# Bidirectional hybrid encoder, two layers on one core: the SSD's heads begun evenly over the short conv's triples, and the FFN's normalized input made pair by pair between the scaled pairs

## The chip, the cores and the metric

The kernel runs on one core of a Trainium2 chip. A core has five engines, each with a queue of its own that it works through in order: TensorE (PE in the profile, with its weight loads shown as PEld), VectorE (DVE), ScalarE (ACT), GpSimd (POOL) and SyncE (SP), which here only issues DMAs. Engines wait for one another through semaphores. The metric is the device time of one execution in microseconds. Three runs of the kernel before gave 796.75 to 798.28 us, with a median of 798.2 us.

## The reference, cut to what matters

The sequence has 256 tokens of 1024 features; there are two layers, and everything is float32.

```python
for l in range(2):
    n = rms_norm(h, norm1_w[l])
    z, xbc, dt_f, dt_b, sc_b, sc_c, sc_v = split(n @ w_in[l])
    y_ssd = ssd_branch(z, xbc, dt_f, dt_b, ...)      # 16 heads in 4 groups, forward and backward, gated, group norm
    y_sc  = sc_b * dwconv3(sc_c * sc_v, sc_conv_w[l])  # the short conv
    h = h + concat(y_ssd, y_sc) @ w_out[l]
    n = rms_norm(h, norm2_w[l])
    g, u = split(dwconv3(n @ w_ffn_up[l]) + ffn_conv_b[l])   # 2816 columns each
    h = h + (silu(g) * u) @ w_ffn_down[l]
out = rms_norm(h, final_norm_w)
```

## The kernel before

Activations lie with features on the 128 partitions and the 256 tokens along the row. Every large product is made from three matmuls: the operands are split into a high and a low part in the engine's reduced float32 (`hilo`, L101 to L103: ACT writes the high part, DVE subtracts it for the low part), and high x high, low x high and high x low are added up in PSUM. Weights come as chunks of 128x1024: SP loads one into a `raw` buffer, ACT makes `wh` (L102), DVE makes `wl` (L103), four chunks ahead of use; there are seven buffers of `wh` and `wl`, so a chunk's split waits until PE has used the seventh before it. 128 matmul columns of an input projection are one half of a **pair**; a pair has 48 matmuls of 256 columns, works off two chunks (24 matmuls each: the first uses input features 0 to 511, the second 512 to 1023), and fills one of four PSUM banks named `mm`.

**The norm.** RMSNorm needs the sum over all features before its factor `rs` is known. So the first pairs of each projection are multiplied from the unnormalized input times the norm's weight (`hwh`, `hwl`), and their result is scaled afterwards by DVE (`take`, which writes `u`); these are the scaled pairs. Once `rs` is there, `normed` makes the normalized input: for each of four feature pairs p, two DVE multiplications `nf` of 128x256, one ACT cast `nh` and one DVE subtraction `nl` of 128x512. Pairs from index NU = 5 on (6 in the first layer's mixer) take `nh` and `nl`. In an FFN, pairs 0 to 2 lie around the computation of `rs`, pairs 3 and 4 are scaled pairs too, and pair 5 is the first that reads `nh` and `nl`. `Norm.some` makes one feature pair; it is also handed to `pair` as `between`, which calls it behind each half of a scaled pair. In the kernel before, `scale` empties `left` at once for all norms but the first layer's mixer, and the later calls of `some` find nothing to do. Each FFN pair has two column blocks, gate and up: `conv` (one ACT and two DVE instructions each, `cacc`), a SiLU `sg` on ACT, and the product `af` on DVE.

**The mixer's second half.** The short conv's twelve pairs come as four triples (c, v, b). Beside them DVE and ACT work on the SSD's 16 heads; `HEADS_AT` is made from the table `_STARTS`, which names for each head the slot at which it begins, with two slots to a pair (2n + 1 for pair n) and, from 24 on, one slot to each chunk of the output projection. Four heads make a group: the first one of a group issues its transposes and score products on PE (`xp`, `sp`), each head makes its decay matrix `m` on DVE, and HEAD_LAG = 4 slots behind the group's last head PE multiplies (`py`). Then DVE adds up the group (L723 to L730) and splits its square sum (`sqx`), and NORM_LAG = 4 slots later PE sums it over the partitions (`gt`), which the group's norm needs.

**The order.** A scheduler lays the instructions of each engine in a row from the program's order and its own estimate of when each is ready. On the engine, that row is fixed.

Of the kernel before, what the change touches and what calls it, by code (L numbers as in the profile page):

```python
# [42 lines left out]
DT_BASE = 3072  # L43


_STARTS = (1, 3, 3, 7, 9, 11, 11, 15, 17, 19, 19, 21, 21, 23, 24, 24)
HEADS_AT = {_n: _STARTS.count(_n) for _n in _STARTS}
HEAD_LAG = 4
NORM_LAG = 4
# [17 lines left out]
def hybrid_trunk(ctx: ExitStack, tc: tile.TileContext, xT, w_in, w_dt, w_out, w_up, w_dn,  # L67
# [100 lines left out]
    def chunk():  # L168
        while len(split) < min(len(plan), pos[0] + 1 + AHEAD):
            issue()  # L170
        got = split[pos[0]]
        split[pos[0]] = None
        pos[0] += 1
        return got
# [30 lines left out]
    def begin():  # L205
# [29 lines left out]
        for q in range(4):  # L235
            if q > 1:
                square(q - 2)
            hi, lo = parts("hwh"), parts("hwl")
            for j in range(2):
                if q == 0 and j == 0:  # L240
                    raw, wh, _ = w(0, 0)
                    put(v, v.tensor_copy(wh, raw))
                scale = x0[:, 2 * q + j:2 * q + j + 1]
                put(s, s.activation(hi[:, j, :], h[q][:, j, :], AF.Identity, scale=scale))
                put(v, v.scalar_tensor_tensor(out=lo[:, j, :], in0=h[q][:, j, :], scalar=scale,
                                              in1=hi[:, j, :].bitcast(F32), op0=ALU.mult, op1=ALU.subtract))
                xs.append((hi[:, j, :], lo[:, j, :]))
            for i in range(BEGIN):
                raw, wh, wl = w(i, q)
                if q or i:  # L250
                    put(s, s.copy(wh, raw))
                put(v, v.tensor_tensor(out=wl, in0=raw, in1=wh.bitcast(F32), op=ALU.subtract))
            if q == 1:

                gate = const.tile([P, 1], F32, name="gate")
                put("pool", nc.gpsimd.tensor_copy(gate, lo[:, 1, 0:1].bitcast(F32)))
# [33 lines left out]
    def scaled(l):  # L290

        for i, (name, n) in enumerate(NORMS.items()):
            w = x0[:, 0:KD] if l == 0 and name == "n1" else pars[l][:, COL[name]:COL[name] + 8]
            a = s.activation(wn[l][:, i], w, AF.Identity, scale=-0.5 / n)
            if l:
                after(a, tab["uses"][-1])
# [8 lines left out]
    def products(ps, wts, xs, first, last, js=None):  # L305

        wh, wl, kc, cols = wts
        for kk in range(kc):
            xh, xl = xs[kk]
            for j in js or range(cols // P):  # L310
                o = kk * cols + j * P
                a, b = wh[:, o:o + P], wl[:, o:o + P]
                f = first and kk == 0
                e = last and kk == kc - 1
                te.matmul(ps[:, j, :], a, xh, start=f and j == 0, stop=False, skip_group_check=True)
                te.matmul(ps[:, j, :], a, xl, start=False, stop=False, skip_group_check=True)
                te.matmul(ps[:, j, :], b, xh, start=False, stop=e, skip_group_check=True)

    def first_pairs(xs):

        ps = [ps_mm.tile([P, 2, L], F32, name="mm") for _ in range(BEGIN)]
        wts = [[chunk(), chunk()] for _ in range(BEGIN)]
        for q in range(4):
            for ab in (((0, 0), (0, 1)), ((1, 0),)):
                for i, (a, b) in ((i, x) for i in range(BEGIN) for x in ab):
                    for k in (2 * q, 2 * q + 1):
                        for j in range(2):
                            o = k % KC * 256 + j * P
                            te.matmul(ps[i][:, j, :], wts[i][k // KC][a][:, o:o + P], xs[k][b],
                                      start=k == 0 and j == 0 and a == b, stop=k == KD - 1 and a == 1, skip_group_check=True)  # L330
        return ps

    def pair(xs, between=lambda k: None):
        ps = ps_mm.tile([P, 2, L], F32, name="mm")
        n = len(xs)
        for k in range(0, n, KC):
            products(ps, chunk(), xs[k:k + KC], k == 0, k + KC >= n)
            between(k)
        return ps
# [11 lines left out]
    def exact(sq):  # L351

        t = k2("sqx", F32R)
        hilo(sq, t[:, 0, :], t[:, 1, :])
        return t[:, 0, :], t[:, 1, :]

    def halves_sum(sq):
        r = k1("sqh")
        v.tensor_tensor(out=r, in0=sq[:, 0, :], in1=sq[:, 1, :], op=ALU.add)
        return r  # L360

    def rstd(sq, n, name, sq_on):

        tot = bank(name)[:, 0, :]
        for i, x in enumerate(sq):
            te.matmul(tot, ones_r, x, start=i == 0, stop=i == 1)
        r = tmp.tile([P, L], F32, name="rs1") if name == "tot" else k1("grs")
        return newton(tot, n, k1("ry"), k1("rt"), r, sq_on)
# [13 lines left out]
    def weighted(l, name, pairs):  # L382

        xs = []
        for p in pairs:
            hi, lo = parts("hwh"), parts("hwl")
            for j in range(2):
                w = pc(l, name, 2 * p + j)
                s.activation(hi[:, j, :], h[p][:, j, :], AF.Identity, scale=w)
                v.scalar_tensor_tensor(out=lo[:, j, :], in0=h[p][:, j, :], scalar=w,  # L390
                                       in1=hi[:, j, :].bitcast(F32), op0=ALU.mult, op1=ALU.subtract)
                xs.append((hi[:, j, :], lo[:, j, :]))
        return xs
# [13 lines left out]
    class Norm:  # L407
# [10 lines left out]
        def begin(self, pairs):  # L418
            self.raw += weighted(self.l, self.name, pairs)
            for p in pairs:  # L420
                self.sq = squares(p, h[p], self.sq)

        def scale(self):
            if self.l == 0 and self.name == "n1":
                scaled(0)
            self.r = rstd(exact(halves_sum(self.sq)), D, "tot", v)
            self.full, self.left = [], [0, 1, 2, 3]
            if self.l or self.name != "n1":
                while self.left:
                    self.some()  # L430

        def some(self, go=True):

# [13 lines left out]
        def pairs(self, extra=None):  # L447

            first = self.rest is None

            def more():
                if extra is not None:
                    for k in range(0, KD, KC):
                        extra(k)
            if first:
                ps = first_pairs(self.raw)
                more()
                ps += [pair(self.raw, lambda k: self.scale() if k == 0 else self.some())]
            else:

                ps = [ps_mm.tile([P, 2, L], F32, name="mm") for _ in range(2)]
                for i, c in ((0, 0), (1, 0), (0, 1), (1, 1)):
                    if (i, c) == (1, 1):
                        more()
                    products(ps[i], chunk(), self.raw[KC * c:KC * c + KC], c == 0, c == 1)
                    if (i, c) == (0, 0):
                        self.rest()
                        self.begin((2, 3))
                if extra is not None:
                    self.scale()  # L470
                else:
                    ps += [pair(self.raw, lambda k: self.scale() if k == 0 else None)]
            for x in ps:
                yield self.take(x, True)
            nu = NU_FIRST if first else NU
            for n in itertools.count(len(ps)):
                yield self.take(pair(self.raw, self.some) if n < nu else pair(self.full), n < nu)

    def across(acc, x, wts, c, half, first=False):
# [485 lines left out]
```

## Time and profile before

| | before |
|---|---|
| median of three runs | 798.2 us (796.75 to 798.28) |
| the profiled execution's own time | 797.5 us |
| its span, first to last instruction | 795.7 us |
| PE busy | 785.3 us (99%) |
| DVE busy | 652.6 us (82%) |
| ACT busy | 536.6 us (67%) |

The times that follow count from the start of the span. A matmul's length in the profile overlaps the next one's; what PE spends on a run of matmuls is best read from the chain, as start and length of the whole run. Two DVE instructions that don't wait overlap by about 0.08 us in the profile as well, so a row of them costs its length less that much each.

### The profile page before, as it was taken

How to read it: one execution, taken by the hardware profiler on the slowest of the kernel's cores; microseconds unless marked ns; L12 is line 12 of the kernel's file. 1: busy time of each engine (PE TensorE's matmuls, PEld its weight loads, DVE VectorE, ACT ScalarE, POOL GpSimd, SP SyncE). 2: the span in 40 equal slices, each digit the busy share in tenths (PEclk: the TensorE clock that was granted, in tenths of full speed). 3: DMA queues.
4: the chain of work that ended last, by engine and by line, in shares of the span. 5: the costliest groups of instructions: out<-in, count | busy, mean ns of one | idle time of the engine just before them, and what ended most of it. 6: DMA issues, size and time to landing. Idle time of an engine off the chain costs nothing.

```text
span 795.7 us, 14870 instructions
## 1 busy us (share of the span) xinstructions
PE 785.3 (99%) x5730; PEld 742.9 (93%) x5730; DVE 652.6 (82%) x1106; ACT 536.6 (67%) x962; POOL 39.0 (5%) x68
## 2 busy tenths in 40 slices
PE   9999999999999999999999999999999999999996
PEld 9999999978999999999899999999889999999995
DVE  7997879998699977777599778899968999777773
ACT  7866968986766655555577679789747665555552
POOL 1002201100000000000000102101000000000000
PEclk9999999999999999999999999999999999999998
DMA  8568676556454776655373876656656348565531
GB/s 293 192 202 309 175 248 213 174 161 232 123 180 134 245 227 188 185 186 185 113 238 100 257 240 207 215 183 188 185 181 202 117 160 263 187 185 186 185 107 54
DMA packets 47463, 151.31 MB, mean 190 GB/s; under 512 B 9104, under 2 KB 9936, under 8 KB 47392
## 3 DMA queue, kind: packets, MB, share of 16 engines
q1 hardware_dynamic: 39680, 138.98, 54.3%
q0 software_dynamic: 7424, 10.99, 4.8%
q8 instruction: 45, 0.74, 0.4%
q10 hardware_dynamic: 288, 0.39, 0.1%
q14 instruction: 26, 0.21, 0.1%
HBM read 149.14 MB, written 1.15 MB: 189 GB/s over the span
## 4 chain that ended last, share of the span: by engine, by line
PE 92%; DVE 5%; ACT 1%; issue 1%; DMA 0%; DVEq 0%; ACTq 0%
PE mm L95 72%; PE dn L95 15%; PE py L95 2%; DVE wl L103 1%; DVE nf L398 1%; PE sp L95 1%; ACT wh L102 1%; PE warm L95 1%; PE tr L99 1%; DVE w L649 0%; DMA raw<-in_w_out_dram 0%; PE dtp L95 0%; DVE nl L103 0%; PE xp L99 0%; DVE m L651 0%
## 5 line engine op out<-in xcount | busy, mean ns | idle before, releaser
L102 ACT CAST wh<-raw 128x1024 fp32r<-128x1024 f32 (+1 forms) x259 | 267.6, 1039 | 175.8 <-PE mm L95 99.7
L103 DVE TENSOR_TENSOR wl<-raw,wh 128x1024 fp32r<-128x1024 f32 (+1 forms) x257 | 311.8, 1216 | 86.3 <-ACT wh L102 86.1
L95 PE MATMUL mm<-nh,wh 128*128 128x256 f32 x1136 | 323.1, 284 | 0.0
L95 PE MATMUL mm<-nh,wl 128*128 128x256 f32 x1136 | 321.5, 283 | 0.0
L95 PE MATMUL mm<-nl,wh 128*128 128x256 f32 x1136 | 321.4, 283 | 0.0
L95 PEld LDWEIGHTS mm<-nl,wh 128*128 128x128 f32 x1136 | 217.8, 192 | 1.4
L95 PEld LDWEIGHTS mm<-nh,wh 128*128 128x128 f32 x1136 | 217.7, 192 | 1.4
L95 PEld LDWEIGHTS mm<-nh,wl 128*128 128x128 f32 x1136 | 217.8, 192 | 0.1
L95 PE MATMUL mm<-hwh,wh 128*128 128x256 f32 x336 | 91.9, 285 | 0.9 <-DVE u L444 0.9
L95 PE MATMUL mm<-hwl,wh 128*128 128x256 f32 x336 | 91.2, 283 | 0.0
L95 PE MATMUL mm<-hwh,wl 128*128 128x256 f32 x336 | 90.5, 283 | 0.0
L95 PE MATMUL dn<-wh,acth 128*128 128x512 f32 x176 | 69.1, 392 | 0.0
L95 PE MATMUL dn<-wh,actl 128*128 128x512 f32 x176 | 68.9, 391 | 0.0
L95 PE MATMUL dn<-wl,acth 128*128 128x512 f32 x176 | 68.5, 389 | 0.0
L95 PEld LDWEIGHTS mm<-hwh,wh 128*128 128x128 f32 x336 | 62.6, 192 | 1.4 <-PE mm L95 1.3
L95 PEld LDWEIGHTS mm<-hwl,wh 128*128 128x128 f32 x336 | 62.3, 190 | 0.1
L95 PEld LDWEIGHTS mm<-hwh,wl 128*128 128x128 f32 x336 | 62.1, 190 | 0.0
L95 PE MATMUL mm<-wh,mixh 128*128 128x512 f32 x128 | 50.5, 395 | 0.7 <-DVE sy L794 0.7
L95 PE MATMUL mm<-wl,mixh 128*128 128x512 f32 x128 | 49.9, 390 | 0.0
L95 PE MATMUL mm<-wh,mixl 128*128 128x512 f32 x128 | 49.9, 390 | 0.0
L516 DVE SCALAR_TENSOR_TENSOR cacc<-mm,pars,cacc 128x255 f32<-128x255 f32 x88 | 42.0, 477 | 4.6 <-ACT cacc L515 4.4
L518 DVE SCALAR_TENSOR_TENSOR cacc<-mm,pars,cacc 128x255 f32<-128x255 f32 x88 | 42.3, 481 | 2.4
(177 smaller groups left out, 936.7 us busy)
## 6 DMA issues: line engine op xcount, KB each, us to landing
raw<-in_w_in_dram SPq DMA_DIRECT2D x91, 512.0 KB, 4.4
raw<-in_w_up_dram SPq DMA_DIRECT2D x88, 512.0 KB, 3.9
raw<-in_w_dn_dram SPq DMA_DIRECT2D x44, 512.0 KB, 3.6
raw<-in_w_out_dram SPq DMA_DIRECT2D x32, 512.0 KB, 4.2
bc<-dcs POOLq DMA_DIRECT2D x32, 256.0 KB, 5.5
raw<-in_w_in_dram SPq DMA_DIRECT2D x10, 256.0 KB, 5.1
er<-der POOLq DMA_DIRECT2D x16, 128.0 KB, 5.9
h<-in_xT_dram SPq DMA_DIRECT2D x3, 256.0 KB, 5.7
```

Source lines behind the costliest of these rows:

```text
L95: cls.put(nc.tensor.matmul(*args, **kw))
L99: cls.put(nc.tensor.transpose(*args))
L102: s.copy(hi, full)
L103: v.tensor_tensor(out=lo, in0=full, in1=hi.bitcast(F32), op=ALU.subtract)
L398: v.scalar_tensor_tensor(out=n[:, j, :], in0=h[p][:, j, :], scalar=wc(l, name, 2 * p + j), in1=r, op0=ALU.mult, op1=ALU.mult)
L516: v.scalar_tensor_tensor(out=acc[:, 1:L], in0=u[:, 0:L - 1], scalar=w0, in1=acc[:, 1:L], op0=ALU.mult, op1=ALU.add)
L518: v.scalar_tensor_tensor(out=acc[:, 0:L - 1], in0=u[:, 1:L], scalar=w2, in1=acc[:, 0:L - 1], op0=ALU.mult, op1=ALU.add)
```

## The change

The table of starts is replaced by one in which the heads begin evenly, the last at slot 21 in place of 24. And `scale` no longer empties `left`: the normalized pairs are made by the calls of `some` between the halves of the scaled pairs, with a loop that makes what is left before the first full pair.

```diff
-_STARTS = (1, 3, 3, 7, 9, 11, 11, 15, 17, 19, 19, 21, 21, 23, 24, 24)
+_STARTS = (1, 3, 3, 5, 7, 7, 9, 11, 11, 13, 15, 15, 17, 19, 19, 21)
...
             self.full, self.left = [], [0, 1, 2, 3]
-            if self.l or self.name != "n1":
-                while self.left:
-                    self.some()
...
             nu = NU_FIRST if first else NU
             for n in itertools.count(len(ps)):
+                if n >= nu:
+                    while self.left:
+                        self.some()
                 yield self.take(pair(self.raw, self.some) if n < nu else pair(self.full), n < nu)
```

The number of matmuls and of DMAs stays as it was, and SP's queue is the same row for row. What moves is shown at three places.

**The first FFN, DVE, behind `rs`.** Before, the four normalized pairs stand right behind the norm's factor, and the first `u` behind the third `nl`:

```order
L379 SCALAR_TENSOR_TENSOR rs_3050<-rt,ry 128x256
L398 SCALAR_TENSOR_TENSOR nf<-x_84,wn_90,rs_3050 128x256 x2
L398 SCALAR_TENSOR_TENSOR nf<-h_85,wn_90,rs_3050 128x256 x2
L103 TENSOR_TENSOR nl<-nf,nh 128x512
L398 SCALAR_TENSOR_TENSOR nf<-h_86,wn_90,rs_3050 128x256
L103 TENSOR_TENSOR nl<-nf,nh 128x512
L398 SCALAR_TENSOR_TENSOR nf<-h_86,wn_90,rs_3050 128x256
L398 SCALAR_TENSOR_TENSOR nf<-h_87,wn_90,rs_3050 128x256 x2
L103 TENSOR_TENSOR nl<-nf,nh 128x512
L444 SCALAR_TENSOR_TENSOR u<-mm,rs_3050 128x512
```

Now the first `u` stands right behind `rs`, and the FFN's own work on pairs 0 to 2 follows, with five weight chunks among it:

```order
L379 SCALAR_TENSOR_TENSOR rs_3050<-rt,ry 128x256
L441 SCALAR_TENSOR_TENSOR u<-mm,rs_3050 128x512
L103 TENSOR_TENSOR wl<-raw,wh 128x1024
L516 SCALAR_TENSOR_TENSOR cacc<-u,pars_88,cacc 128x255 x2
L518 SCALAR_TENSOR_TENSOR cacc<-u,pars_88,cacc 128x255 x2
L103 TENSOR_TENSOR wl<-raw,wh 128x1024
L856 SCALAR_TENSOR_TENSOR af<-cacc,pars_88,sg 128x256
L441 SCALAR_TENSOR_TENSOR u<-mm,rs_3050 128x512 x2
L103 TENSOR_TENSOR wl<-raw,wh 128x1024
L516 SCALAR_TENSOR_TENSOR cacc<-u,pars_88,cacc 128x255 x2
L518 SCALAR_TENSOR_TENSOR cacc<-u,pars_88,cacc 128x255 x2
L103 TENSOR_TENSOR wl<-raw,wh 128x1024
```

**The same row of DVE, a little further on**, directly behind the piece above (of the second `af` to the second pair's `nl`):

```order
L856 SCALAR_TENSOR_TENSOR af<-cacc,pars_88,sg 128x256
L516 SCALAR_TENSOR_TENSOR cacc<-u,pars_88,cacc 128x255 x2
L103 TENSOR_TENSOR actl<-af,acth 128x512
L518 SCALAR_TENSOR_TENSOR cacc<-u,pars_88,cacc 128x255 x2
L103 TENSOR_TENSOR wl<-raw,wh 128x1024
L856 SCALAR_TENSOR_TENSOR af<-cacc,pars_88,sg 128x256
L398 SCALAR_TENSOR_TENSOR nf<-x_84,wn_90,rs_3050 128x256 x2
L398 SCALAR_TENSOR_TENSOR nf<-h_85,wn_90,rs_3050 128x256 x2
L103 TENSOR_TENSOR nl<-nf,nh 128x512
L441 SCALAR_TENSOR_TENSOR u<-mm,rs_3050 128x512
L103 TENSOR_TENSOR nl<-nf,nh 128x512
```

The first `nl` has moved behind three `u`, twelve `cacc`, three `af`, one `actl` and five `wl`. The third one follows that piece after another 13 instructions: three more `nf` with the first of them ahead of four `cacc`, an `af`, a `u`, a `wl`, an `actl` and one `cacc`:

```order
L398 SCALAR_TENSOR_TENSOR nf<-h_86,wn_90,rs_3050 128x256
L516 SCALAR_TENSOR_TENSOR cacc<-u,pars_88,cacc 128x255 x2
L518 SCALAR_TENSOR_TENSOR cacc<-u,pars_88,cacc 128x255 x2
L398 SCALAR_TENSOR_TENSOR nf<-h_86,wn_90,rs_3050 128x256
L856 SCALAR_TENSOR_TENSOR af<-cacc,pars_88,sg 128x256
L398 SCALAR_TENSOR_TENSOR nf<-h_87,wn_90,rs_3050 128x256 x2
L441 SCALAR_TENSOR_TENSOR u<-mm,rs_3050 128x512
L103 TENSOR_TENSOR wl<-raw,wh 128x1024
L103 TENSOR_TENSOR actl<-af,acth 128x512
L516 SCALAR_TENSOR_TENSOR cacc<-u,pars_88,cacc 128x255
L103 TENSOR_TENSOR nl<-nf,nh 128x512
```

On ACT, the last two `nh` now stand behind the split of the chunk `wh` that needs the buffer of pair 5's first half:

```order
L139 ACTIVATE sg<-cacc,pars_88 128x256
L102 CAST wh<-raw 128x1024
L102 CAST acth<-af 128x512
L515 ACTIVATE cacc<-u,pars_88 128x256 x2
L102 CAST nh<-nf 128x512 x2
```

**The first mixer, DVE, the last group's square sum.** Before, the rows ahead of the last but one group's `sqx` (x_1081 and x_1153 are the third and fourth group's sums) read:

```order
L103 TENSOR_TENSOR wl<-raw,wh 128x1024
L730 TENSOR_TENSOR sq<-sq 128x256
L723 TENSOR_TENSOR yo<-py,er 128x256
L724 SCALAR_TENSOR_TENSOR x_1153<-x_1153,pars_88,py 128x256
L723 TENSOR_TENSOR yo<-py,er 128x256
L726 TENSOR_TENSOR x_1153<-x_1153,yo 128x256
L103 TENSOR_TENSOR sqx<-sq,sqx 128x256
```

Now the last group's stands there:

```order
L103 TENSOR_TENSOR wl<-raw,wh 128x1024
L726 TENSOR_TENSOR x_1153<-x_1153,yo 128x256
L103 TENSOR_TENSOR wl<-raw,wh 128x1024
L727 TENSOR_TENSOR x_1153<-x_1153,z_859 128x512
L103 TENSOR_TENSOR wl<-raw,wh 128x1024
L730 TENSOR_TENSOR sq<-sq 128x256
L103 TENSOR_TENSOR wl<-raw,wh 128x1024 x2
L103 TENSOR_TENSOR sqx<-sq,sqx 128x256
```

On PE, the product `gt` that needs this last `sqx` now comes two matmuls (one `gt`) behind the place where the third group's came before; in between lies the same work. The second layer's mixer and FFN have the same rows at these places.

## Rows read from the trace of the kernel before

**Rows 1.** The page, busy time, share of the span and count of each engine.

```profile
PE 785.3 (99%) x5730; PEld 742.9 (93%) x5730; DVE 652.6 (82%) x1106; ACT 536.6 (67%) x962; POOL 39.0 (5%) x68
```

**Rows 2.** The waits of PE: for whom, us in total, times, longest.

```profile
PE gt L95 <- ACT sqx L102: 1.1, 1, 1.1
...
PE mm L95 <- DVE u L444: 0.9, 2, 0.5
PE mm L95 <- DVE sy L794: 0.7, 1, 0.7
```

**Rows 3.** The chain that ended last, pieces by start and length: PE's runs.

```profile
83.55 0.44 PE xp L99 x4
...
233.23 17.49 PE mm L95 x144
...
412.69 63.35 PE mm L95 x528
...
623.31 17.51 PE mm L95 x144
```

**Rows 4.** The timeline of DVE in the first FFN: start, length, line, instruction.

```profile
226.95 0.42 DVE L379 SCALAR_TENSOR_TENSOR rs<-rt,ry 128x256 f32<-128x256 f32 x1
227.41 0.88 DVE L398 SCALAR_TENSOR_TENSOR nf<-x,wn,rs 128x256 f32<-128x256 f32 x2
...
229.00 0.69 DVE L103 TENSOR_TENSOR nl<-nf,nh 128x512 fp32r<-128x512 f32 x1
...
232.39 0.69 DVE L444 SCALAR_TENSOR_TENSOR u<-mm,rs 128x512 f32<-128x512 f32 x1
...
233.59 1.22 DVE L103 TENSOR_TENSOR wl<-raw,wh 128x1024 fp32r<-128x1024 f32 x1
234.73 0.88 DVE L516 SCALAR_TENSOR_TENSOR cacc<-u,pars,cacc 128x255 f32<-128x255 f32 x2
...
237.74 0.48 DVE L856 SCALAR_TENSOR_TENSOR af<-cacc,pars,sg 128x256 f32<-128x256 f32 x1 [0.21 <-ACT sg L139]
...
243.71 0.69 DVE L103 TENSOR_TENSOR actl<-af,acth 128x512 fp32r<-128x512 f32 x1
```

**Rows 5.** The timeline of ACT in the first FFN.

```profile
228.33 0.62 ACT L102 CAST nh<-nf 128x512 fp32r<-128x512 f32 x1 [0.28 <-DVE nf L398]
...
245.88 1.05 ACT L102 CAST wh<-raw 128x1024 fp32r<-128x1024 f32 x1 [1.49 <-DMA raw<-in_w_up_dram]
246.96 0.91 ACT L515 ACTIVATE cacc<-u,pars 128x256 f32<-128x256 f32 x2
...
251.03 0.61 ACT L102 CAST acth<-af 128x512 fp32r<-128x512 f32 x1
```

**Rows 6.** The chain's first pieces: PE's first matmuls.

```profile
1.06 5.07 PE warm L95 x22
```

**Rows 7.** Windows: the two mixers' second halves in two parts each, and the end.

```profile
core 0: us, PE busy (x) PEld busy (x) DVE busy (x) ACT busy (x) POOL busy (x), PEclk, DMA share, GB/s
101.00:135.80 34.80, 34.80 (x293) 34.29 (x292) 28.65 (x54) 26.26 (x58) 4.37 (x7) 1.00 0.71 228
135.80:179.80 44.00, 42.25 (x300) 37.15 (x298) 43.65 (x98) 37.82 (x89) 4.68 (x8) 1.00 0.57 180
488.70:528.00 39.30, 39.30 (x333) 38.84 (x332) 35.19 (x69) 31.28 (x71) 4.95 (x8) 1.00 0.75 237
528.00:569.60 41.60, 41.60 (x300) 37.44 (x299) 41.11 (x91) 36.57 (x84) 4.67 (x7) 1.00 0.56 169
789.20:791.40 2.20, 0.00 (x0) 0.00 (x0) 1.33 (x5) 1.19 (x5) 0.00 (x0) 1.00 0.00 0
791.40:793.00 1.60, 0.00 (x0) 0.00 (x0) 0.52 (x1) 0.58 (x1) 0.00 (x0) 0.51 0.12 48
```

**Rows 8.** The timeline of DVE around the third group's `sqx`, both mixers.

```profile
179.39 0.42 DVE L103 TENSOR_TENSOR sqx<-sq,sqx 128x256 fp32r<-128x256 f32 x1 [0.34 <-ACT sqx L102]
...
569.15 0.42 DVE L103 TENSOR_TENSOR sqx<-sq,sqx 128x256 fp32r<-128x256 f32 x1 [0.47 <-ACT sqx L102]
```

**Rows 9.** The timeline of PE: the third group's `gt`, second mixer.

```profile
569.94 0.40 PE L95 MATMUL gt<-sqx,ones_r 128*128 128x256 f32 x2
```

**Rows 10.** The timeline of DVE in the second layer's mixer, the norm's factor.

```profile
415.65 0.43 DVE L379 SCALAR_TENSOR_TENSOR rs<-rt,ry 128x256 f32<-128x256 f32 x1
```

## Prediction

> **What bounds the kernel now.** I read the busy times first. PE works 785.3 of a span of 795.7 us, DVE 652.6, ACT 536.6 [rows 1]: PE sets the time, and an edit counts only where it lets PE stand or takes a stand away. The waits of PE come next [rows 2]: one of 1.1 us for the square sum of an SSD group, two for a `u` (0.9 together, the longer 0.5) and one of 0.7 for `sy`. So at most about 2.7 us can be won at these places. Then the chain [rows 3]: around each FFN's start it is DVE's norm for some 6 us, then PE without a stop for 144 matmuls, three pairs of 5.8 us, from 233.23 and from 623.31. The first of them is pair 4, which needs the bank that the first `u` empties; the second is pair 5, the first that reads `nh` and `nl`. DVE and ACT in that stretch give the durations [rows 4, 5].
>
> **The FFN's norm.** Nothing is taken away; the order says what is late next. Before, `u` stood behind three normalized pairs and ended 0.45 us late for pair 4 [rows 2]. Now it stands directly behind `rs`, and that wait goes: pair 4 starts at about 232.8 and pair 5 wants its input at 238.5, one pair (5.75) later.
>
> DVE's row from `rs` to the first `nl` holds, by the order, 3 `u`, 5 `wl`, 12 `cacc`, 3 `af`, 1 `actl`, 4 `nf` and the `nl`. Each costs its length less the overlap of 0.08 us [rows 4]: 3 x 0.61 + 5 x 1.14 + 12 x 0.395 + 3 x 0.40 + 0.60 + 4 x 0.40 + 0.60 = 16.3 us. `rs` is done at 227.4, so the first `nl` is done at 243.7, even if DVE never waits. **PE stands 5.2 us ahead of pair 5's first half.** The second `nl` follows after one `u` (244.9), in time for its twelve matmuls. The half ends at 246.6 (half a pair, 2.9 us). The second half needs the third `nl`: from the first `nl` on 2 `u` (1.22), the second `nl` (0.60), 4 `nf` (1.60), 5 `cacc` (1.98), an `af` (0.40), a `wl` (1.14), an `actl` (0.60) and itself (0.60), 8.1 us in all, so 251.8. **PE stands another 5.2 us.** The fourth `nl` is done by 252.8, in time. Pair 5 ends at 251.8 + 2.9 = 254.7; before it ended at 233.23 + 11.5 = 244.7. That is +10.0 us for an FFN, the gain of 0.45 counted in it, and the second FFN has the same rows and the same 144 matmuls: **+20 us**.
>
> Two bounds. From below: the 16.3 hold no wait of DVE, and before it waits in this stretch for ACT (0.21 us ahead of an `af` [rows 4]), so the stands are hardly shorter; an engine's row is fixed. From above: on ACT the last two `nh` stand behind the split of a chunk whose buffer pair 5's first half frees at 246.6; from there `wh` 0.97, `acth` 0.55, two `cacc` 0.8, `nh` 0.55 [rows 5] give about 249.5, ahead of what DVE needs, so nothing is added unless PE's first half is late. Waits of DVE for chunks and for ACT may add 0.5 a stand: 9 to 11 an FFN. Later pairs are not behind: while PE stands, DVE and ACT work off what they would have done beside pairs 5 and 6.
>
> **The clock.** Before, PE never stood longer than 1.1 us [rows 2], and the granted clock is 1.00 in every stretch of [rows 7] in which it works. At the end PE stops at 789.2; the clock is 1.00 in the next 2.2 us and 0.51 in the 1.6 after [rows 7]: a stand of 5 us is long enough for it to fall from 2.4 to 1.2 GHz. At the start, 22 matmuls of 128x128 on a clock not yet raised take 5.07 us, 0.23 each [rows 6], where four of the same size take 0.44, 0.11 each, later [rows 3]. So after such a stand PE may work for up to 5.07 us at half pace and lose half of it, 2.5 us. Behind the first stand that is partly covered: the half takes up to 5.8 instead of 2.9 us and ends at 249.5, still ahead of 251.8, but the split that ACT has ahead of the last two `nh` comes 2.9 later, and the third `nl` with it at about 253: +1.2. Behind the second, up to 2.5 uncovered. Between 0 and 3.7 an FFN; I take 2.5, since the stands are more than twice the 2.2 us after which the end shows the fall: **+5 us** in all. The Trainium skill ("TensorE: Matmul & The Clock Gate", What's actually happening) calls the slow clock the default, which activity releases; by that the sum would keep these 5 us, as it does by the rows. If the clock stays at 1.00, the sum is without them.
>
> **The heads.** Up to `wl` at about 98 us DVE's row is the same as before. From there before reaches the third group's `sqx`, at 179.39 and 569.15 [rows 8], and its `gt`; the change has the last group's `sqx` there, behind more of the heads' work, and the `gt` that needs it one `gt` (0.24 us) later on PE. By the rows of the order that is one `wl` (1.14), two 128x512 (1.2 as `nl`) and eight 128x256 (8 x 0.36, between `sqx` less the overlap and `cacc`) more: 5.2 us, less the 0.24: 5.0. What can hide it is idle time of DVE early in the half, which the heads are to fill: 34.80 - 28.65 = 6.15 us in the first mixer up to 135.8 and 39.30 - 35.19 = 4.1 in the second up to 528.0; behind these, DVE is full (43.65 of 44.00, 41.11 of 41.60) [rows 7]. If none is filled, +5.0 in the first mixer, and +4.6 in the second, where `gt` ran at 569.94 [rows 9], 0.4 behind its operand. If all is filled, the first gains the 1.1 that PE waits there [rows 2], and the second gains nothing, since PE does not wait: 5.0 - 0.4 - 4.1 leaves +0.5. I take two thirds filled, as rows that wait for chunks and for PE's products don't move freely: 5.0 - 4.1 = 0.9 and 4.6 - 2.7 = 1.9, so **+3 us** (-0.6 to +9.6). The first mixer's 0.7 for `sy` [rows 2] I leave where it is. On POOL two loads of a head's rows change places; at nothing, because a head's start at the earlier slot takes its load with it.
>
> **The second mixer's norm** is moved in the same way, but has slack: `rs` at 415.65 [rows 10], the first `nl` about 10 us later (3 `u`, 8 `cacc`, 6 `nf`, one `wl`, two short `dv`), ACT included by 427; pair 5 comes at 412.69 + 3 x 5.75 = 429.9 [rows 3]. The third `nl` at about 430 is ahead of 432.8. Zero; if its cover of 3 us goes, each late us is one of PE. The first mixer's norm did not empty `left` in `scale` and stays.
>
> **Sum.** 797.5 (the profiled execution) + 20 + 5 + 3 = 825.5; the median of the runs is 0.7 above that execution: 826.
>
> **Rivals.**
> 1. *The clock holds* in all four stands: 826 - 5 = 821. For it: the wait is cut in two by 2.9 us of full work. Against it: the end of this trace.
> 2. *DVE's idle time is not filled*: the heads cost 9.6 instead of 3, 832.5. For it: before, DVE's idle pieces there end with a chunk, whose time PE sets. Against it: heads that begin earlier have operands that do not hang on these chunks.
> 3. *The second stand stays out*: PE's first stand gives ACT and DVE time to catch up, if the rows between the two `nl` cost 2.9 instead of 8.1; the FFNs then cost 2 x 4.8 and 2 x 1.2 for the clock, 797.5 + 9.6 + 2.4 + 3 + 0.7 = 813. Against it: those 13 rows need 8.1 without any wait.
> 4. *Faster*: the early `u` is what counts. PE loses its 0.9 for `u`, the even heads take the 1.1 away, and `nl` is in time: 798.2 - 2 = 796. It decides at 238.5: DVE would have to get from `rs` to the first `nl` in 11.1 us, and 16.3 stand there. For it are only the waits named; I give it 5 in 100.
>
> **How the numbers follow.** Clock falls, idle filled by two thirds: 0.55, 826 (821 to 831, the heads and the clock at their nearer ends). Rival 1: 0.25, 821. Rival 2: 0.10, 832.5. Rival 3: 0.05, 813. Rival 4: 0.05. What a measurement of this kernel can tell from no change is about 0.2%, 1.6 us; slower by more than that are all but the last: 0.93, with 0.02 between and 0.05 faster. The range reaches from rival 3 less 2 to the upper end of the unfilled heads with the clock's full 3.7 an FFN (832.5 + 2.4, with 2 for waits): 811 to 837.
>
> **What the changed profile would show.** Right: `u` directly behind `rs`, and no wait for it; two waits of PE of about 5 us in each FFN, around 238 to 244 and 247 to 252 (later by what the first mixer adds; some 390 us on for the second), ended by `nl` or `nh`; a granted clock below 1.00 in the stretch behind them; one or two waits of `gt` of 1 to 3 us in the mixers; none at pair 5 of the second mixer. Wrong: PE without a stop from pair 4 to pair 6 (the row of DVE costs less than I add up), a clock of 1.00 there, waits of `py` or `sp` for heads in the mixers, or a wait at the second mixer's pair 5.

## The result and the profile after

The changed kernel takes 836.1 us in the median of four runs (831.7 to 838.0), where the kernel before took 797.5 in the four runs beside it (796.1 to 798.3): a ratio of 1.048 (95% interval 1.043 to 1.052), or 38.6 us more. The forecast was 826 us, with 811 to 837 as its range. The profiled execution has a span of 836.3 us, 40.6 more than before, and is the longest of the four.

The page of the changed kernel, its busy times, which answer to [rows 1]:

```profile
PE 801.8 (96%) x5730; PEld 757.4 (91%) x5730; DVE 658.3 (79%) x1106; ACT 535.1 (64%) x962; POOL 39.0 (5%) x68
```

PE does the same 5730 matmuls and is busy 16.5 us longer: it worked a part of them at a lower clock. A stand is time in which PE has nothing that it may start. The waits of PE in the changed kernel (for whom, us in total, times, longest), beside [rows 2]:

```profile
PE mm L95 <- ACT nh L102: 15.7, 4, 5.0
PE py L95 <- DVE m L651: 6.9, 3, 2.8
PE mm L95 <- DVE sy L794: 2.7, 2, 1.3
PE mm L95 <- DVE nl L103: 1.4, 4, 0.6
```

The two waits for `u` and the one for `sqx` are gone. In their place stand 17.1 us for the normalized input and 9.6 us in the mixers, for `m` and `sy`. DVE's timeline in the first FFN of the changed kernel (start, length, line, instruction) shows why, from `rs` to the third `nl`, beside [rows 4]:

```profile
234.50 0.43 DVE L379 SCALAR_TENSOR_TENSOR rs<-rt,ry 128x256 f32<-128x256 f32 x1
234.96 0.69 DVE L441 SCALAR_TENSOR_TENSOR u<-mm,rs 128x512 f32<-128x512 f32 x1
...
249.50 0.88 DVE L398 SCALAR_TENSOR_TENSOR nf<-x,wn,rs 128x256 f32<-128x256 f32 x2
...
251.08 0.68 DVE L103 TENSOR_TENSOR nl<-nf,nh 128x512 fp32r<-128x512 f32 x1
...
259.88 0.69 DVE L103 TENSOR_TENSOR nl<-nf,nh 128x512 fp32r<-128x512 f32 x1
```

`u` stands directly behind `rs`; the first `nl` starts 16.2 us behind `rs` and ends at 251.8, 16.8 behind. PE's timeline of the changed kernel at the same place (a bracket holds the idle time ahead and what ended it):

```profile
245.80 0.28 PE L95 MATMUL mm<-hwh,wl 128*128 128x256 f32 x1
251.08 0.58 PE L95 MATMUL mm<-nh,wh 128*128 128x256 f32 x1 [5.00 <-ACT nh L102]
...
256.05 0.34 PE L95 MATMUL mm<-nh,wl 128*128 128x256 f32 x1
...
259.60 0.58 PE L95 MATMUL mm<-nh,wh 128*128 128x256 f32 x1 [2.85 <-ACT nh L102]
260.62 0.58 PE L95 MATMUL mm<-nl,wh 128*128 128x256 f32 x1 [0.44 <-DVE nl L103]
```

Pair 4 ends at 246, PE stands 5 us, works the first half of pair 5 in 5.5 us in place of 2.9, and stands 3.3 us again. The windows of the changed kernel (busy time and count of each engine, then the granted clock, the DMA share and GB/s) say what it worked at, here and in the first mixer:

```profile
148.00:152.00 4.00, 0.61 (x4) 0.40 (x6) 4.00 (x11) 4.00 (x14) 0.55 (x1) 0.79 0.50 135
152.00:156.00 4.00, 4.00 (x21) 3.67 (x20) 3.20 (x9) 4.00 (x10) 0.00 (x0) 0.50 0.50 139
...
247.00:250.00 3.00, 0.00 (x0) 0.00 (x0) 3.00 (x7) 0.93 (x2) 0.00 (x0) 0.89 0.39 156
250.00:253.00 3.00, 1.76 (x6) 1.47 (x7) 3.00 (x7) 1.83 (x4) 0.00 (x0) 0.50 0.57 175
253.00:256.00 3.00, 3.00 (x16) 3.00 (x15) 2.88 (x8) 0.82 (x2) 0.00 (x0) 0.50 0.01 3
256.00:259.00 3.00, 0.74 (x6) 0.53 (x4) 2.60 (x5) 2.34 (x5) 0.00 (x0) 0.97 0.00 0
259.00:262.00 3.00, 1.97 (x7) 1.68 (x8) 2.96 (x7) 1.57 (x4) 0.00 (x0) 0.59 0.56 171
262.00:265.00 3.00, 3.00 (x16) 3.00 (x15) 0.95 (x2) 0.00 (x0) 0.00 (x0) 0.50 0.01 4
```

The granted clock was 0.50, the lower of its two levels (1.2 in place of 2.4 GHz), behind each stand of the FFN, and, which the forecast did not have, behind two stands in the mixer. Taken by stretches between the factors `rs`, the 40.6 us of the span are: 7.5 up to the first FFN's `rs` (234.50 against 226.95), 13.6 from there to the second mixer's (436.84 against 415.65), 5.5 to the second FFN's (643.68 against 617.04) and 14.0 from there to the end. So the FFNs' stretches lost 27.6 where 25 were forecast, and the heads 13.0 where it was 3.

The stands in the mixer are those of `py`, the third group's products. PE's timeline of the kernel before has it here:

```profile
163.08 1.09 PE L95 MATMUL py<-m,xt 128*64 128x128 f32 x16
```

and that of the changed kernel here:

```profile
145.69 0.66 PE L95 MATMUL py<-m,xt 128*64 128x128 f32 x8
148.62 0.40 PE L95 MATMUL py<-m,xt 128*64 128x128 f32 x2 [2.27 <-DVE m L651]
151.79 1.11 PE L95 MATMUL py<-m,xt 128*64 128x128 f32 x6 [2.77 <-DVE m L651]
```

The group's first product comes 17.4 us earlier than before (145.69 against 163.08): its last head begins at slot 15 in place of 21, three pairs earlier. PE is at the group's third `m` at 148.62 - 2.27 = 146.35, 16.7 us ahead of the time at which the products began before. The last of the four, the twelfth `m` of the mixer, came only 6.1 earlier. DVE's timeline before, and then of the changed kernel:

```profile
157.43 0.40 DVE L651 TENSOR_TENSOR m<-e,w 128x256 f32<-128x256 f32 x1
```

```profile
148.06 0.42 DVE L651 TENSOR_TENSOR m<-e,w 128x256 f32<-128x256 f32 x1
...
151.32 0.42 DVE L651 TENSOR_TENSOR m<-e,w 128x256 f32<-128x256 f32 x1
```

Before, the last `m` was done 163.08 - 157.8 = 5.2 us ahead of the first product. 16.7 - 6.1 - 5.2 = 5.4 us are missing, and 2.27 + 2.77 = 5.04 is what PE stood, with two matmuls in between.

### The profile page after: what moved, and what is told of

It reads as the page before. It is cut to its first block, busy times and chain, and to the rows that moved or that the text cites. A ratio compares the mean times of both kernels' runs of the same rounds, so it can differ in the third digit from the quotient of the medians.

```text
span 836.3 us, 14884 instructions
## 1 busy us (share of the span) xinstructions
PE 801.8 (96%) x5730; PEld 757.4 (91%) x5730; DVE 658.3 (79%) x1106; ACT 535.1 (64%) x962; POOL 39.0 (5%) x68
## 4 chain that ended last, share of the span: by engine, by line
PE 75%; ACT 8%; DVE 8%; DMA 6%; issue 2%; SPq 0%; DVEq 0%; ACTq 0%
PE mm L95 58%; PE dn L95 15%; DMA raw<-in_w_in_dram 5%; ACT wh L102 2%; ACT e L643 2%; DVE wl L103 2%; PE py L95 2%; ACT w L648 1%; DVE cacc L516 1%; DMA raw<-in_w_out_dram 1%; ACT cacc L515 1%; DVE nf L398 1%; DVE cacc L518 1%; DVE nl L103 1%; PE tr L99 1%
## 5 line engine op out<-in xcount | busy, mean ns | idle before, releaser
L95 PE MATMUL mm<-nh,wh 128*128 128x256 f32 x1136 | 329.6, 290 | 15.7 <-ACT nh L102 15.7
L95 PE MATMUL mm<-nl,wh 128*128 128x256 f32 x1136 | 327.6, 288 | 1.4 <-DVE nl L103 1.4
L95 PE MATMUL mm<-nh,wl 128*128 128x256 f32 x1136 | 326.8, 288 | 0.1
L95 PEld LDWEIGHTS mm<-nh,wh 128*128 128x128 f32 x1136 | 223.7, 197 | 17.9 <-ACT nh L102 16.5
L95 PEld LDWEIGHTS mm<-nl,wh 128*128 128x128 f32 x1136 | 223.6, 197 | 3.8 <-DVE nl L103 2.5
L95 PEld LDWEIGHTS mm<-nh,wl 128*128 128x128 f32 x1136 | 223.5, 197 | 0.3 <-DVE wl L103 0.3
```

The costliest lines, as they stand in the source:

```text
L95: cls.put(nc.tensor.matmul(*args, **kw))
```

## The experiments

**The two parts alone.** The first has only the new table:

```diff
-_STARTS = (1, 3, 3, 7, 9, 11, 11, 15, 17, 19, 19, 21, 21, 23, 24, 24)
+_STARTS = (1, 3, 3, 5, 7, 7, 9, 11, 11, 13, 15, 15, 17, 19, 19, 21)
```

> Only the table of starts is new; the norm is as before. The sum on record gives the heads +3 us: about 800.5. The changed kernel's profile says otherwise: up to the factor rs of the first FFN it is 7.5 us behind, from the second mixer's rs to the second FFN's another 5.5. If these are the heads alone, 797.5 + 13 = 810.5, with PE standing for m at py by 5.0 and 1.9 us and for sy by 1.3 in each mixer, and no stand in the FFNs but the two for u. If the FFNs' late norm had a part in them, less than 805.

Measured: 809.3 us, ratio 1.0153 (1.0131 to 1.0175) against 797.2. The waits of PE with the table alone:

```profile
PE py L95 <- DVE m L651: 6.3, 3, 2.5
PE mm L95 <- DVE sy L794: 2.7, 2, 1.3
...
PE mm L95 <- DVE u L444: 1.0, 2, 0.5
```

The heads alone cost 12.1 us, four times the term on record, and at the places that the changed kernel shows. The second has only the norm:

```diff
             self.full, self.left = [], [0, 1, 2, 3]
-            if self.l or self.name != "n1":
-                while self.left:
-                    self.some()
...
+                if n >= nu:
+                    while self.left:
+                        self.some()
```

> Only the norm is made pair by pair; the starts are as before. On record: +20 for the stands and +5 for the clock, 822.5. The changed kernel's profile gives 13.6 and 14.0 for the two stretches that begin at the FFNs' rs: 797.5 + 27.6 = 825. In both cases PE stands 5 us for the first nh or nl of pair 5 and 3 to 5 for the third, in each FFN, and the mixers have their 1.1 for sqx and 0.7 for sy as before. If the two parts disturb each other, this one and the heads alone do not add up to the 38.6 us of the whole.

Measured: 823.5 us, 1.0327 (1.0304 to 1.0349), 26.3 us more than before, between the two numbers expected. 12.1 + 26.3 = 38.4 against the 38.6 of the whole: within the noise the parts don't disturb each other. The third has the starts of before and keeps the norm of before in the FFNs, so that only the second mixer's is made pair by pair. It adds this to the version with the norm alone:

```diff
+            if self.name == "n2":
+                while self.left:
+                    self.some()
```

> The norm pair by pair in the second layer's mixer alone; the FFNs' and the heads are as before. On record this costs nothing, since the first nl is there at about 427 and wanted at 429.9: 797.2, no stand at pair 5 of that mixer. If 3 us of cover are too few (ACT's chunks ahead of the last nh), PE stands there by what is over, 799 or more.

Measured: 797.6 us, 1.0003 (0.9989 to 1.0016). As on record, nothing.

**The clock.** To the norm alone, matmuls whose result nobody reads were added where PE stands:

```diff
+                if n == nu and self.name == "n2":
+                    idle = bank("idle")
+                    def keep(k):
+                        if k == 0:
+                            for _ in range(40):
+                                te.matmul(idle[:, 0, :], ones_r, self.raw[0][0], start=True, stop=True)
+                    keep(0)
+                    yield self.take(pair(self.full, keep), False)
+                    continue
```

> The norm pair by pair, and 40 matmuls of 128x256 whose result is not used ahead of each half of the FFNs' pair 5 (about 4.8 us each at full clock), so that PE works through most of its stands. If the clock is what the stands cost beyond their length, the granted clock stays at 1.00 and each FFN loses only its two stands, 10 us less the 0.45: 797.5 + 20 = 817.5, some 7 us below the norm without these matmuls. If the extra 7 us are DVE's or ACT's, the time stays at that kernel's 825; if the matmuls only lengthen PE's work, it is above.

Measured: 817.5 us, 1.0251 (1.0226 to 1.0275), 6.0 less than the norm alone with 160 matmuls more. DVE's row is the same in both. PE's timeline with the added matmuls, first FFN:

```profile
238.85 4.95 PE L95 MATMUL idle<-hwh,ones_r 128*128 128x256 f32 x40
243.96 0.39 PE L95 MATMUL mm<-nh,wh 128*128 128x256 f32 x1 [0.16 <-ACT nh L102]
244.70 0.39 PE L95 MATMUL mm<-nl,wh 128*128 128x256 f32 x1 [0.35 <-DVE nl L103]
...
247.56 4.96 PE L95 MATMUL idle<-hwh,ones_r 128*128 128x256 f32 x40
253.01 0.38 PE L95 MATMUL mm<-nl,wh 128*128 128x256 f32 x1 [0.37 <-DVE nl L103]
```

The stretch around the stands in windows, first without the added matmuls and then with them:

```profile
240.00:266.00 26.00, 19.51 (x112) 18.24 (x113) 20.87 (x38) 12.33 (x22) 0.00 (x0) 0.80 0.27 84
```

```profile
240.00:266.00 26.00, 25.11 (x194) 24.02 (x193) 23.07 (x43) 14.21 (x25) 0.00 (x0) 1.00 0.31 103
```

The clock is at 1.00 in place of 0.80. What is left, 817.5 - 797.2 = 20.3 us, are the stands themselves. In this timeline the two halves of pair 5, from the end of the work before to their own end, take 5.8 and 5.4 us more than their 24 matmuls need. So the 6.0 are the clock's. The Trainium skill ("TensorE: Matmul & The Clock Gate", HAM oscillation — how this bites in real kernels) tells of a matmul kernel in which each wait for a DMA makes the next piece of work start at the low clock; this pair of runs agrees, with 3.0 us an FFN.

**The deadline of pair 5.** The norm pair by pair again, with two more scaled pairs in the FFNs, so that pair 7 is the first that reads `nh` and `nl`:

```diff
-            nu = NU_FIRST if first else NU
+            nu = NU_FIRST if first else NU + 2 * (self.name == "n2")
```

> The norm pair by pair, with pairs 5 and 6 of the FFNs scaled ones too, so that pair 7 is the first that reads nh and nl. By the order and the durations read, pair 7 begins 11.1 + 11.5 + 2.8 = 25.4 us behind rs and needs the first nl then (there at 16.8) and the third at 28.3 (there at about 26): no stand, the clock at 1.00, and the two waits for u gone: 797.5 - 0.9 = 796.6. If the loss is not the deadline of pair 5 but DVE's work being in a worse order altogether, PE stands somewhere else behind rs, for cacc, actl or a chunk, and the time is above 800.

Measured: 796.0 us, 0.9989 (0.9973 to 1.0004). All waits of PE for an FFN's norm are gone, for `u` as for `nl`:

```profile
PE gt L95 <- ACT sqx L102: 2.3, 1, 2.3
PE warm L95 <- DVE eps L278: 1.1, 1, 1.1
PE mm L95 <- DVE wl L103: 0.5, 1, 0.5
```

DVE's late `nl` costs nothing when the pair that reads it is two later: the loss in the FFNs is this deadline and not the work.

**Which heads.** Only the first eight begin early:

```diff
+_STARTS = (1, 3, 3, 5, 7, 7, 9, 11, 17, 19, 19, 21, 21, 23, 24, 24)
```

> The evenly begun starts for heads 0 to 7 alone; heads 8 to 15 begin at the slots of before (17 to 24). If the loss sits in the third and fourth group, whose work now falls beside the short conv's triples where DVE is full, it is gone: within 2 us of before, 797, and the idle 6 us of DVE up to 136 us are used. If beginning early itself costs, by the early heads' rows in front of chunks, part of the 12 us stays: above 801.

Measured: 796.6 us, 0.9996 (0.9983 to 1.0009); in the mixers' second halves PE waits 0.4 us for one `sqx` and for nothing else. The first eight heads cost nothing when they begin early. The window of this version up to 136 us shows that DVE's idle time there takes them:

```profile
101.00:135.80 34.80, 34.80 (x302) 34.08 (x302) 32.65 (x64) 26.97 (x57) 5.80 (x9) 1.00 0.77 243
```

32.65 us busy against 28.65 [rows 7]. The changed kernel itself has less of it filled there, with all heads begun early:

```profile
101.00:135.80 34.80, 34.80 (x300) 33.98 (x300) 30.84 (x64) 29.29 (x70) 5.24 (x9) 1.00 0.73 214
```

Then the first twelve:

```diff
+_STARTS = (1, 3, 3, 5, 7, 7, 9, 11, 11, 13, 15, 15, 21, 23, 24, 24)
```

> The evenly begun starts for heads 0 to 11; the fourth group's heads begin at 21 to 24 as before. If the third group's early products (py at slot 19 in place of 25) are the loss, PE still stands for their m, 2 to 4.4 us in the first mixer, and most of the 12 us stays: 804 to 809. If it is the fourth group's rows in front of the third's m and of sy, the stands go and the time is 797 to 799.

Measured: 814.3 us, 1.0226 (1.0209 to 1.0242), more than with all sixteen. Only the third group's starts differ from the version with the first eight (796.6), so it is the third group that costs, and the fourth group's rows are not what delays it. Why it costs 5 to 6 us more here than with all sixteen stays open. PE's timeline in the first mixer:

```profile
152.10 0.66 PE L95 MATMUL py<-m,xt 128*64 128x128 f32 x2 [5.35 <-DVE m L651]
154.14 1.11 PE L95 MATMUL py<-m,xt 128*64 128x128 f32 x6 [1.38 <-DVE m L651]
```

**Where PE multiplies them.** With the same starts, the third group's `py` alone was put two pairs later:

```diff
-                later(slot + HEAD_LAG, products_of(hd, state["grp"], head(hd, state["bc"].pop(0), tok, state["grp"])))
+                later(slot + HEAD_LAG + (4 if hd // HPG == 2 else 0), products_of(hd, state["grp"], head(hd, state["bc"].pop(0), tok, state["grp"])))
```

> As the version with the evenly begun starts for heads 0 to 11 (814.3), but PE multiplies the third group (py) 8 slots behind its heads in place of 4: at slot 23, two pairs or 11.5 us later, still one pair earlier than before (25). Its heads begin as early as there. There PE stood 5.4 + 1.4 us for its m in the first mixer, 3.6 + 1.4 in the second. If PE's product placed too early is the loss, all of these are shorter than 11.5 us and go: 797 to 799. If it is the heads' own rows on DVE and ACT, which stay where they are, cv, sy or a chunk is late in their place and the time stays above 803.

Measured: 801.2 us, 1.0033 (1.0017 to 1.0050), above the 797 to 799 expected. The kernel before took 798.1 beside it, so 3.0 us are left of the 17.9 that the first twelve cost against theirs (796.4). No wait for `m` is left; in place of the 0.7 for `sy` in the first mixer [rows 2] there is now a longer one in each mixer:

```profile
PE mm L95 <- DVE sy L794: 4.0, 2, 2.6
```

In the first mixer, DVE's timeline has the rows of the third group's sum directly ahead of this `sy`, from `yo` on, and PE's has the stand:

```profile
163.39 0.42 DVE L723 TENSOR_TENSOR yo<-py,er 128x256 f32<-128x256 f32 x1
...
165.17 0.41 DVE L794 TENSOR_TENSOR sy<-mm,cacc 128x256 f32<-128x256 f32 x1
```

```profile
166.31 0.50 PE L95 MATMUL mm<-wh,mixh 128*128 128x512 f32 x1 [2.60 <-DVE sy L794]
```

These rows last 1.8 us, where PE stands 2.6.

And all heads even, with every group's `py` one pair later:

```diff
-HEAD_LAG = 4
+HEAD_LAG = 6
```

> The heads alone, and HEAD_LAG 6 in place of 4: PE multiplies a group (py) one pair, 5.75 us, later behind its last head, and the group's sum moves with it. In the profile of the heads alone PE stands 4.4 us for the third group's m in the first mixer and 1.9 in the second. If the loss is that py of the third group comes too early for DVE's row, these stands are shorter than the 5.75 us, go, and the clock stays at 1.00: 798 to 801, with the 1.3 for sy at most. If the loss is that the heads delay the splits of the chunks (their wl and so their DMAs and ACT), py's place is indifferent, PE stands as long for a wl or for sy, and the time stays near 809.

Measured: 803.9 us, 1.0087 (1.0062 to 1.0112), 7.1 more than the 796.8 beside it: some 5 of the 12 us are gone, not nearly all of them, and none of the waits for `m` is left. The waits moved to the start of the output projection:

```profile
PE mm L95 <- DVE sy L794: 5.4, 2, 3.2
PE mm L95 <- DVE cv L789: 1.9, 1, 1.9
PE mm L95 <- DVE wl L103: 1.5, 1, 1.5
```

Both say that a part of the loss is the place of the third group's `py`, which is too early: 14.9 of 17.9 us with the first twelve early, some 5 of 12 with all of them. Behind it lies a second part. The later sums of the heads then stand on DVE ahead of the short conv's last rows, for which the output projection waits; for `sy` the rows above show it, for `cv` and `wl` it is inferred.

**Less work for DVE, a test that did not decide.** The even heads, with two products of each group (`xg`, and the gate `z`) on GpSimd:

```diff
-        v.tensor_tensor(out=xg, in0=xt.rearrange("p (c f x) -> p c f x", c=2, f=HPG),
+        nc.gpsimd.tensor_tensor(out=xg, in0=xt.rearrange("p (c f x) -> p c f x", c=2, f=HPG),
...
-                v.tensor_tensor(out=xs[g], in0=xs[g], in1=feat["z", g], op=ALU.mult)
+                nc.gpsimd.tensor_tensor(out=xs[g], in0=xs[g], in1=feat["z", g], op=ALU.mult)
```

> The heads alone, with two instructions of each group on GpSimd in place of DVE (xg, and the product with the gate z, 128x512 each, 0.6 us on DVE): about 3 to 3.6 us less of DVE's row up to the third group's py in a mixer, same schedule of heads. If the stands are DVE's full row, the 4.4 us for m in the first mixer fall to 1 or 2, the second mixer's 1.9 goes, the clock holds better, and the time falls from 809 to about 801 to 803. If ACT behind late chunks is what sets m, DVE's relief changes nothing, 809; more than that if GpSimd's slower products are waited for.

Measured: 818.8 us, 1.0282 (1.0261 to 1.0303), 22.4 more than the kernel before beside it, where the heads alone cost 12.1. GpSimd's two instructions as groups (length in ns: least, median, most):

```profile
L629 POOL TENSOR_TENSOR xg<-xt,gtok x8: 1038/1041/1215, 91.0 to 548.8; 128x512 f32<-128x512 f32 x8
```

```profile
L727 POOL TENSOR_TENSOR x<-x,z x8: 1316/2702/3337, 119.6 to 584.9; 128x512 f32<-128x512 f32 x8
```

The gate's product takes 2.7 us there, 0.68 on DVE, and it lies on the way to `sqx`, for which PE now stands 3.6 us. The wait for `m` in the first mixer is 1.9 + 2.1, hardly less than 1.9 + 2.5. DVE had less to do, but stood itself, 1.8 us of it for `sq`, which ACT makes from the gate's product. So this run does not tell whether DVE's amount of work sets the third group's `m`, or ACT, which in the changed kernel has two chunks that land late in its row ahead of these heads (its timeline):

```profile
138.49 1.04 ACT L102 CAST wh<-raw 128x1024 fp32r<-128x1024 f32 x1 [1.70 <-DMA raw<-in_w_in_dram]
141.73 1.05 ACT L102 CAST wh<-raw 128x1024 fp32r<-128x1024 f32 x1 [2.20 <-DMA raw<-in_w_out_dram]
```

The changed kernel's trace answers a part of it. Between 131.4 and 151.7 us, up to the end of the twelfth `m`, DVE is busy for 19.47 of 20.38 us, and its only wait is one for ACT's `sq`, which stands behind the second of these chunks:

```profile
143.34 0.42 DVE L730 TENSOR_TENSOR sq<-sq 128x256 f32<-128x256 f32 x1 [0.91 <-ACT sq L729]
```

So in this stretch ACT's late chunks delay DVE by at most 0.9 of the 5.0 us, and the rest is DVE's own full row. What put so much into that row ahead of the `m`, and whether another order would have done, no run here tells.

**A version below both.** The later pair 7, the starts of before, and `gt` one slot later:

```diff
-NORM_LAG = 4
+NORM_LAG = 5
```

> Two things put together to get below before: the norm pair by pair with pairs 5 and 6 of the FFNs scaled ones (796.0 alone, no stand in the FFNs), the starts of before, and NORM_LAG 5 in place of 4, so that gt comes one chunk later than the third group's sqx, for which PE stood 2.3 us there. If that stand goes and none takes its place: 796.0 - 2.3 = 793.7. If the later norm of a group makes mixl late for the output projection, the wait turns up there and the time is 796 or above.

Measured: 794.8 us, 0.9973 (0.9960 to 0.9986): 0.3% less than before (796.8 beside it), and the only version whose interval lies below 1. PE's waits are down to 0.9 for `wl` and 0.5 for `sy`. Against the version with the later pair 7 alone (0.9989, 0.9973 to 1.0004) the gain of the later `gt` is not clear of the noise. With the early first eight heads as well:

> The version with the later pair 7 and NORM_LAG 5 (794.8), with the evenly begun starts for heads 0 to 7 as well, which took the stands for sqx and sy from 1.7 to 0.4. What is left to win at PE's stands are the 0.5 for sy and 0.9 for wl: 793.5 to 794.8; over 796 if the early heads and the later norm of a group collide.

Measured: 796.9 us, 1.0006 (0.9994 to 1.0017). The two collide: the waits for `sy`, 0.5 without the early heads, are 2.1 us with them.

## Why the prediction was right, point by point

**The FFN's stands** came as summed. The row of DVE to the first `nl` was put at 16.3 us and took 16.8; the stands at 5.2 and 5.2, and with the clock held they are 5.8 and 5.4. The 20 us on record are 20.3 in the run with the added matmuls.

**The clock** fell, as the likeliest case had it. 5 us were on record, 6.0 are what holding it gives back. The way was the one described: the first half of pair 5 at half pace is covered in part by the second stand, which shrinks to 3.3 us. One of its witnesses is weaker than it reads: for the kernel's first 5 us, in which the prediction calls the clock not yet raised [rows 6], the profile gives a granted clock of 1.00, so that the half pace there rests on the lengths of the matmuls alone. Behind the stands the windows show 0.50 themselves. Rival 1, that the clock holds, is refuted, and so is rival 3.

**The second mixer's norm** costs nothing, as on record: the first `nl` was done 9.8 us behind `rs`.

**The heads** were mis-sized, 3 us on record against 12.1, and the step that failed can be named. The step took the last group's `sqx` and its `gt` for the deadline, and asked how much of the 5 us more on DVE would be hidden ahead of it. But the same table moves `py` on PE: the third group's went 17.4 us forward, its last `m` 6.1. That wait was named among the signs of a wrong forecast and not priced, though the trace of before has the slack, 5.2 us (157.8 to 163.08), and the table the three pairs by which `py` moves. The wait for `gt` that was priced is not there at all. Nor was a clock below 1.00 in the mixers counted: the stands of 2.27 and 2.77 us brought it to 0.50, as the windows show. And of DVE's idle 6.15 us [rows 7] about a third was filled in the changed kernel (30.84 us busy in 101.0 to 135.8, from 28.65), not two thirds.

That the total came out inside the range is in part luck. The heads' own bounds were -0.6 to +9.6 us, and 12.1 lies outside them; the sum stayed under 837 because its upper end also held 7.4 us for the FFNs' clock, where 6.0 were needed, and 2 for waits. One of the four runs, 838.0, lies above it.

**Rival 2** had the size, 832.5 us, but another mechanism. **Rival 4**, that the early `u` is what counts, has a small truth: the waits for `u` and `sqx` [rows 2] are gone, 2.0 us, and a version that is rid of them without the new stands is at 794.8.

## What to carry to other kernels

When a table moves the start of some work, list every later instruction that it moves with it on every engine, and compare for each how far the consumer moved with how far the operand moved; here one such pair, the third group's `py` and its last `m`, shows the 5 us of stands in the first mixer. The rest of the 12.1 (the second mixer's stand, the waits for `sy`, the clock behind them) comes on top of it. A stand costs more than its length when the clock falls behind it, so one that can't be removed may be worth filling with matmuls, as the 6.0 us show. And work that is late for its first reader need not be made earlier: it may be enough that the reader comes later, as with pair 7 in place of pair 5.

## What the runs showed of the hardware that was not expected

The clock also fell behind stands half as long as the FFN's. In the first mixer of the changed kernel there were two of 2.27 and 2.77 us, with two matmuls between them, and it was at 0.50 in the next 4 us. It need not be two: in the version that puts the third group's `py` 8 slots behind its heads, the single stand of 2.60 us was followed by 0.50 from 168 to 170 us. The stand of 2.3 us for `sqx` in the version with the later pair 7, and those of up to 1.1 us in the kernel before, left it at 1.00. And a 128x512 product takes GpSimd 1.04 us in one place (`xg`) and 1.3 to 3.3 us in another (the gate), while DVE needs 0.68 for either. The Trainium skill ("SBUF — State Buffer", SBUF: two separate sides) says that DVE and GpSimd share a pair of ports, and that a DVE instruction with two operands in SBUF and a GpSimd instruction that reads there take turns on it, whole instructions long. The spread would agree with it, but no run here measures that by itself.
